# Seven products for three parts of each down projection, with weight sums on GpSimd

## The chip, the cores and the metric

The kernel runs on one core of a Trainium2 chip. The metric is the device time of one execution in microseconds. A core has a matrix engine (TensorE, PE in the profile; PEld is its weight load), a vector engine (VectorE, DVE), a scalar engine (ScalarE, ACT), GpSimd (POOL) and SyncE (SP), which here only issues DMAs. Each works through its own queue in order; semaphores order them among each other. PE reads operands from the on-chip memory SBUF and accumulates into PSUM banks of 512 fp32 columns.

## What is computed

One decoder layer on x of 512 tokens by 1024 channels, in fp32: a SwiGLU feed-forward (FFN 1), a mixer (three groups of dilated attention heads beside a gated linear recurrence), and a second FFN 2, each between two RMS norms. The change concerns the FFNs alone:

```python
def swiglu(x, w_gate, w_up, w_down):
    return (jax.nn.silu(x @ w_gate) * (x @ w_up)) @ w_down

f = swiglu(rms_norm(h, ffn1_norm_pre[l]), ffn1_w_gate[l], ffn1_w_up[l], ffn1_w_down[l])
h = h + 0.5 * rms_norm(f, ffn1_norm_post[l])
```

The hidden width D_FF is 2816, 22 blocks of 128. The down projection multiplies a 512 x 2816 activation by a 2816 x 1024 weight.

## The kernel before

Every fp32 operand is split into a high part in the format fp32r (ACT copies it) and a low part, the difference (DVE subtracts): `split`, lines 268 to 270. A product is three matmuls, high by high, high by low and low by high; `mm3` and `tokens` write these out.

Weights come from HBM in one stream of 1 MB tiles `raw` (two buffers, `raw_of`, loads issued on SP at L215), in an order that `stream_plan` fixes from the same events that drive the loops. Split weights lie in `w8` buffers (four of 1024 columns, high and low), smaller ones in `w4`.

Each FFN goes through 22 blocks f of the hidden width. For the first ones (five in FFN 1, three in FFN 2) gate and up are ordinary products on 512 columns (L282 to L284). For the others gate and up are computed together by `seven` (lines 583 to 622): the product of 2 x 2 blocks with seven block products instead of eight (Winograd's form of Strassen's scheme). Its inputs are sums of activation quarters, formed once per FFN, and sums of weight quarters, formed for each f by `w_forms` (lines 564 to 581): four DVE adds of 512 columns (L570, L571, L572, L575), then three splits of 1024 and one of 512. Its seven products are 84 matmuls on 256 columns (L594 to L596). The products p1, p6 and p7 go on adding in one PSUM bank; in between ACT copies that bank out (L601), and DVE makes the four results of such copies and other products (L606). `prod` then applies SiLU and the product and splits the result u into the activation tiles `act`.

The down projection is cut along the hidden width in five parts, `FF_PARTS` (four of 4 blocks, one of 6). `down(a, half)` multiplies part a for 512 of the 1024 output columns: for each of four token blocks 12 matmuls on 512 columns (L388 to L390, `tokens`), with the activations as stationary and the weights as moving operand. Its weights are split into the buffers `wd` (two). The result is copied (part 0, L662, ACT) or added (L664, DVE) into the SBUF accumulator `facc`. The halves of a part are spread over the gate/up products of the next part. The last part ends the FFN in `last_product`, with squares, norm and residual.

The order on each engine is set by a planner: it goes through the program with a cost for each instruction, and of the instructions that are ready on an engine by these costs it puts the one with the best priority next. Priority is the place in the program; `high_priority(offset)` moves a block ahead by so many places, here 100 for weights (`AHEAD`) and 200 for evacuations (`EVAC`). On the chip an engine follows that fixed order, and an instruction that isn't ready holds up what is behind it. Tiles of one tag share its buffers, and a new tile waits until the users of an old one are done.

The order of events in an FFN (`ffn_order`, lines 49 to 66) lists `std`, `prep` (the weight forms of one f, one product ahead), `prod` (with the halves of the part before) and `down`.

Of the kernel before, what the change touches and what calls it, by code (L numbers as in the profile page):

```python
# [10 lines left out]
F32 = mybir.dt.float32  # L11
F32R = mybir.dt.float32r
# [4 lines left out]
P = 128  # L17
# [3 lines left out]
NF = 22  # L21
FF_PARTS = ((0, 4), (4, 8), (8, 12), (12, 16), (16, 22))
NSTD = {1: 5, 2: 3}
NG = 3
NH = 4
EPS = 1e-6
# [22 lines left out]
def ffn_order(n):  # L49

    order = [("std", f) for f in range(NSTD[n])]
    early = NSTD[n] >= FF_PARTS[0][1]
    order.append(("prep", NSTD[n]))
    if early:
        order.append(("down", 0, 0))
    for a, (f0, f1) in enumerate(FF_PARTS):
        fs = range(max(f0, NSTD[n]), f1)
        halves = () if a == 0 else (1,) if a == 1 and early else (0, 1)  # L60
        for i, f in enumerate(fs):
            if f + 1 < NF:
                order.append(("prep", f + 1))
            c, k = len(fs), len(halves)
            order.append(("prod", f, a - 1, halves[i * k // c:(i + 1) * k // c]))
    return order


# [5 lines left out]
def stream_plan():  # L74

    plan = []

    def down(n, a, half):
        for kk in range(part_blocks(a)):
            plan.append((("down", n, a, half, kk), 1024))  # L80

    def ffn(n):
        for ev in ffn_order(n):
            if ev[0] == "std":
                plan.append((("gate", n, ev[1]), 1024))
                plan.append((("up", n, ev[1]), 1024))
            elif ev[0] == "prep":
                plan.append((("gu", n, ev[1]), 2048))
            elif ev[0] == "down":
                down(n, *ev[1:])  # L90
            else:
                for half in ev[3]:
                    down(n, ev[2], half)
# [36 lines left out]
    ffn(2)  # L130
    return plan

# [24 lines left out]
def hybrid_layer(ctx: ExitStack, tc: tile.TileContext, xT: bass.AP, xN: bass.AP, wst: bass.AP,  # L157
                 first: bass.AP, rows: bass.AP, consts: bass.AP, bias: bass.AP, out: bass.AP):
    nc = tc.nc
    DVE, ACT, PE = nc.vector, nc.scalar, nc.tensor  # L160
# [234 lines left out]

    def gains(pool, *ids):

        t = pool.tile([P, 2, D], F32, name="gains", tag="wd", bufs=2)
# [162 lines left out]

    spool = [None]

    def w_forms(key):

        with tc.high_priority(offset=AHEAD):
            raw = raw_of(key)
            u0, u1, g0, g1 = (raw[:, i * 512:(i + 1) * 512] for i in range(4))
            s12 = spool[0].tile([P, 2, 512], F32, name="s12", tag="s", bufs=2)
            DVE.tensor_add(s12[:, 1, :], u0, u1)  # L570
            DVE.tensor_add(s12[:, 0, :], s12[:, 1, :], g0)  # L571
            DVE.tensor_add(u0, u0, g0)  # L572
# [50 lines left out]

    def ffn(n, x, r, forms_x, apool, pss):
        t, steps = forms_x
        acts = {}

        def act_at(f):

            if f // 4 not in acts:  # L630
                at = apool.tile([P, 8, T], F32R, name="act", tag="act", bufs=3)
                acts[f // 4] = Act([at[:, j, :] for j in range(4)], [at[:, 4 + j, :] for j in range(4)])
            return acts[f // 4].hi[f % 4], acts[f // 4].lo[f % 4]

        def part(a):
            f0, f1 = FF_PARTS[a]
            his, los = zip(*(act_at(f) for f in range(f0, f1)))
            return Act(his, los)

        def std_out(psg, psu, f):  # L640

            g, u = tmp("g"), tmp("u")
            if r is None:
                ACT.activation(g, psg, AF.Silu)
                DVE.tensor_mul(u, psu, g)
            else:
                DVE.tensor_mul(g, psg, r)
                ACT.activation(g, g, AF.Silu)
                DVE.tensor_mul(u, psu, r)
                DVE.tensor_mul(u, u, g)  # L650
            split(*act_at(f), u)

        def wd():
            return apool.tile([P, 2, 1024], F32R, name="wd", tag="wd", bufs=2)

        def down(a, half):
            ws = [fetch(("down", n, a, half, kk), wd, AHEAD) for kk in range(part_blocks(a))]
            for b in range(4):
                ps, y = acc_ps(), fb(b, FHALVES[half])
                tokens(ps, ws, part(a), b)  # L660
# [2 lines left out]
                else:  # L663
                    DVE.tensor_add(y, ps, y)  # L664

        def prod(f, w, a, hs_):
            g, u = tmp("g"), tmp("u")
            seven(t, w, aux_ps()[:, :HB], [g[:, h] for h in HALVES], [u[:, h] for h in HALVES])
            for half in hs_:
                down(a, half)  # L670
            ACT.activation(g, g, AF.Silu)
            DVE.scalar_tensor_tensor(u, g, -1.0, u, op0=ALU.mult, op1=ALU.mult)
            split(*act_at(f), u)

        keys = [(w, n, i) for i in range(NSTD[n]) for w in ("gate", "up")]
        forms = {}
        for ev in ffn_order(n):
# [6 lines left out]
                if j < len(steps):  # L684
                    steps[j]()
            elif ev[0] == "prep":
                forms[ev[1]] = w_forms(("gu", n, ev[1]))
            elif ev[0] == "down":
                down(ev[1], ev[2])
            else:  # L690
                prod(ev[1], forms.pop(ev[1]), ev[2], ev[3])
        a = len(FF_PARTS) - 1
        return lambda half, kk: ("down", n, a, half, kk), part_blocks(a), part(a)


    def act_two(pool):

        ts = [pool.tile([P, 8, T], F32R, name="act", tag="act", bufs=3) for _ in range(2)]
        return Act([ts[0][:, k, :] for k in range(8)], [ts[1][:, k, :] for k in range(8)])

    def spare(pool):

        def pair():
            t = pool.tile([P, 8, T], F32R, name="act", tag="act", bufs=3)
            return [t[:, 4 * i:4 * i + 4, :].rearrange("p (s k) t -> p s (k t)", s=2) for i in range(2)]

        def one():
            return tx_slot(pool).rearrange("p s k t -> p s (k t)")

        both = []  # L710

        def of_pair():
            if not both:
                both.extend(pair())
            return both.pop(0)

        return [of_pair, of_pair, one, w8]

    ff1 = ExitStack()
    ap1 = ff1.enter_context(tc.tile_pool(name="act1", bufs=1))  # L720
    new_h()
    u1 = act_two(ap1)
    acc = npool.tile([P, T], F32, name="acc", tag="acc", bufs=1)
    warm(eps)

# [31 lines left out]
        if b >= 2:  # L757
            bd1.turn(b - 2)

    last_product(*end1, True, grow1, spare(ap1), block1)  # L760
    ff1.close()


# [226 lines left out]
    with ExitStack() as mx:  # L990
# [144 lines left out]
        for c in range(KC):  # L1135
# [5 lines left out]


    ap2 = ctx.enter_context(tc.tile_pool(name="act2", bufs=1))
    u_t = [ap2.tile([P, 8, T], F32R, name="act", tag="act", bufs=3) for _ in range(2)]
    his, los = ([t[:, 0:4, :], t[:, 4:8, :]] for t in u_t)
# [4 lines left out]
    slots = spare(ap2)  # L1150
# [3 lines left out]
    pss = gemm_first(keys[:NFIRST], u2, [spare(ap2)[2]],  # L1154
                     {3: [lambda: bd2.turn(2)], 4: [lambda: bd2.turn(3)]})
    end2 = ffn(2, u2, None, forms_of(u2, his, los, ap2, True), ap2, pss)
    new_h()
# [57 lines left out]
def _block(key, a):  # L1215
# [3 lines left out]
    if kind in ("down", "out"):  # L1219
        if kind == "out":  # L1220
            w, r0, half = a["w_out"], key[2] * 2 * P, key[1]
        else:
            w, r0, half = a[f"ffn{key[1]}_w_down"], (FF_PARTS[key[2]][0] + key[4] * 2) * P, key[3]
        return w[r0:r0 + 2 * P, half * T:(half + 1) * T].reshape(2, P, T).transpose(1, 0, 2)
    if kind == "gu":
        u, g = (_cols(a[f"ffn{key[1]}_w_{k}"], key[2] * P) for k in ("up", "gate"))
        return np.concatenate([u, g], axis=1)
# [54 lines left out]
```

## Time and profile before

| | |
|---|---|
| median of 3 runs (lowest, highest) | 1245.29 us (1245.27, 1245.92) |
| the profiled execution | 1245.37 us, of which the span is 1243.6 us |
| granted PE clock | 0.998 |
| window 57 to 320 us, the products of FFN 1 | 263.00 us: PE busy 263.00, DVE 200.85, ACT 128.42, POOL 2.91 |
| window 905 to 1218 us, those of FFN 2 | 313.00 us: PE busy 313.00, DVE 233.73, ACT 153.47, POOL 3.43 |

The span runs from the first to the last instruction; the little beside it is start and end. Busy times of an engine in a window are the time in which at least one of its instructions runs. Consecutive matmuls and consecutive DVE instructions overlap by their ends, so what a further one costs is the distance from start to start, not its duration. In the timeline a row is: start, duration, engine, line, operation, output<-inputs by tile names, shapes, count, and in brackets idle time before it with what ended it. In the groups a row ends with busy time, mean duration in ns, and idle time before with the releasers. `w`, `wd`, `raw`, `s` are weight tiles (split, split for down, loaded, sums), `acc` and `aux` are PSUM banks.

### The profile page before, as it was taken

The page shows a single profiled execution, that of the slowest core. Times are in us where ns is not written, and L with a number is a line of the kernel's source. Part 1 is how long each engine was busy: PE and PEld are TensorE (multiplying, and loading weights), DVE is VectorE, ACT ScalarE, POOL GpSimd, SP SyncE. Part 2 cuts the span into 40 slices and gives each one's busy share as a digit, 9 for nine tenths or more (in the row PEclk, how much of TensorE's full clock was granted, in tenths as well). Part 3 has the DMA queues.
Part 4 walks back from the last instruction along what each step waited for, and adds up shares of the span by engine and source line. Part 5 has one row for each costly group of instructions (what it writes and reads, how often), then busy time and mean ns, then how long its engine had stood idle before and what let it go on. Part 6 is the DMA issues. An engine that isn't in the chain of part 4 may idle for free.

```text
span 1243.6 us, 19076 instructions
## 1 busy us (share of the span) xinstructions
PE 1232.1 (99%) x7748; PEld 1117.6 (90%) x7748; DVE 930.4 (75%) x1473; ACT 664.3 (53%) x1100; POOL 26.2 (2%) x51
## 2 busy tenths in 40 slices
PE   9999999999999999999999999999999999999997
PEld 8899999999878899999988887888899999999986
DVE  7996777796576588888575898864798667777755
ACT  7555444455355365666544788734565544445432
POOL 0000000000002000000000000000100000000000
PEclk9999999999999999999999999999999999999999
DMA  6222222235424223222243222224443222222241
GB/s 242 102 79 103 101 102 102 101 126 184 167 90 144 85 95 103 77 89 91 100 172 102 70 99 102 102 102 169 142 130 136 103 103 102 103 103 73 103 182 67
DMA packets 27383, 141.37 MB, mean 114 GB/s; under 512 B 2976, under 2 KB 6176, under 8 KB 13216
## 3 DMA queue, kind: packets, MB, share of 16 engines
q1 hardware_dynamic: 20016, 122.86, 27.9%
q0 software_dynamic: 7280, 17.30, 4.1%
q8 instruction: 60, 0.98, 0.3%
q14 instruction: 27, 0.22, 0.1%
HBM read 129.67 MB, written 6.29 MB: 109 GB/s over the span
## 4 chain that ended last, share of the span: by engine, by line
PE 89%; DVE 6%; ACT 4%; issue 1%; DVEq 0%; ACTq 0%
PE acc L594 11%; PE acc L595 11%; PE acc L596 11%; PE acc L388 7%; PE acc L389 7%; PE acc L390 7%; PE acc L282 6%; PE acc L283 6%; PE acc L284 6%; PE aux L595 3%; PE aux L594 3%; PE aux L596 3%; PE acc L793 1%; PE acc L795 1%; PE acc L794 1%
## 5 line engine op out<-in xcount | busy, mean ns | idle before, releaser
L270 DVE TENSOR_TENSOR w<-raw,w 128x1024 fp32r<-128x1024 f32 (+1 forms) x241 | 257.9, 1074 | 97.2 <-ACT w L269 64.7
L269 ACT ACTIVATE w<-raw 128x1024 fp32r<-128x1024 f32 (+1 forms) x241 | 225.2, 938 | 181.3 <-DVE raw L575 61.0
L594 PE MATMUL acc<-big,w 128*128 128x256 f32 x896 | 255.4, 285 | 0.0
L595 PE MATMUL acc<-big,w 128*128 128x256 f32 x896 | 254.4, 284 | 0.0
L596 PE MATMUL acc<-big,w 128*128 128x256 f32 x896 | 254.1, 284 | 0.0
L594 PEld LDWEIGHTS acc<-big,w 128*128 128x128 f32 x896 | 171.6, 192 | 1.0
L595 PEld LDWEIGHTS acc<-big,w 128*128 128x128 f32 x896 | 171.7, 192 | 0.6
L596 PEld LDWEIGHTS acc<-big,w 128*128 128x128 f32 x896 | 171.7, 192 | 0.0
L601 ACT ACTIVATE c<-acc 128x256 f32<-128x256 f32 x172 | 65.2, 379 | 81.4 <-PE acc L596 78.1
L389 PE MATMUL acc<-wd,act 128*128 128x512 f32 x256 | 99.8, 390 | 0.0
L388 PE MATMUL acc<-wd,act 128*128 128x512 f32 x256 | 99.6, 390 | 0.0
L390 PE MATMUL acc<-wd,act 128*128 128x512 f32 x256 | 99.4, 389 | 0.0
L594 PE MATMUL aux<-big,w 128*128 128x256 f32 x288 | 81.5, 283 | 0.0
L595 PE MATMUL aux<-big,w 128*128 128x256 f32 x288 | 81.5, 283 | 0.0
L596 PE MATMUL aux<-big,w 128*128 128x256 f32 x288 | 81.4, 283 | 0.0
L594 PE MATMUL acc<-tx,w 128*128 128x256 f32 x272 | 77.2, 284 | 0.0
L596 PE MATMUL acc<-tx,w 128*128 128x256 f32 x272 | 77.0, 283 | 0.0
L595 PE MATMUL acc<-tx,w 128*128 128x256 f32 x272 | 77.0, 283 | 0.0
L282 PE MATMUL acc<-big,w 128*128 128x512 f32 x192 | 74.7, 389 | 0.0
L283 PE MATMUL acc<-big,w 128*128 128x512 f32 x192 | 74.7, 389 | 0.0
L284 PE MATMUL acc<-big,w 128*128 128x512 f32 x192 | 74.7, 389 | 0.0
L270 DVE TENSOR_TENSOR w<-s,w 128x1024 fp32r<-128x1024 f32 x52 | 63.7, 1224 | 10.2 <-ACT w L269 10.1
(316 smaller groups left out, 2753.0 us busy)
## 6 DMA issues: line engine op xcount, KB each, us to landing
raw<-in_w SPq DMA_DIRECT2D x110, 1024.0 KB, 4.8
big<-act POOLq DMA_DIRECT2D x6, 512.0 KB, 3.4
gains<-in_rows POOLq DMA_DIRECT2D x5, 512.0 KB, 5.0
h<-in_x SPq DMA_DIRECT2D x8, 256.0 KB, 5.0
h<-in_xn POOLq DMA_DIRECT2D x4, 512.0 KB, 7.6
kept_m<-h POOLq DMA_DIRECT2D x4, 512.0 KB, 2.9
h<-kept_m POOLq DMA_DIRECT2D x4, 512.0 KB, 5.4
kept<-h POOLq DMA_DIRECT2D x4, 512.0 KB, 3.4
```

The costliest lines, as they stand in the source:

```text
L269: ACT.activation(dh, src, AF.Copy)
L270: DVE.tensor_sub(dl, src, dh.bitcast(F32))
L282: PE.matmul(ps, wh, xh, start=first, stop=False)
L283: PE.matmul(ps, wh, xl, start=False, stop=False)
L284: PE.matmul(ps, wl, xh, start=False, stop=last)
L388: PE.matmul(ps, x.hi[k][:, bl], wh, start=k == 0, stop=False)
L389: PE.matmul(ps, x.hi[k][:, bl], wl, start=False, stop=False)
L390: PE.matmul(ps, x.lo[k][:, bl], wh, start=False, stop=k == x.n - 1)
L594: PE.matmul(ps, wh, xh, start=start and k == 0, stop=False, skip_group_check=True)
L595: PE.matmul(ps, wh, xl, start=False, stop=False, skip_group_check=True)
L596: PE.matmul(ps, wl, xh, start=False, stop=k == 3, skip_group_check=True)
L601: ACT.activation(c, ps, AF.Copy)
```

## The change

Parts 1, 2 and 3 of each down product (blocks 4 to 16) are each computed in seven products. A part is taken as 2 x 2 blocks: two token halves of 256 by two halves of its hidden width (256 each) times two by two blocks of weights (256 by 512). `down7` has 7 products of 12 matmuls on 512 columns, in place of 96 such matmuls; the weights move and the activations are stationary, as before.

- Weights of a part come as two 1 MB tiles (`dg`). `d_forms` makes four sums of 1024 columns on GpSimd and seven splits of 1024: four ahead of the gate/up product before, three (`rest`) after the first product of the down7.
- Activation sums are made when the gate/up results come (`into`): for the first two blocks of a part a difference, for the other two three further sums and a split of 1024.
- The bank that p1, p6 and p7 share is added up over the three parts: after each of them its contents are put into SBUF tiles `e` (part 1: ACT copies, later: DVE adds), and four adds of 1024 columns on DVE put them into `facc` at the end of part 3. The other products are added into `facc` directly. That makes 14 evacuations of 512 columns a part, in place of 8.
- The down product of a part now stands in one piece, behind the first gate/up product of the next part (part 0: both halves in a row), and no weight forms of a further gate/up product are made ahead at that place.
- `w_forms` makes its four sums on GpSimd for f from 8 on (`LATE`), on DVE before.
- The activation tiles lie elsewhere: tags `e`, `wd` (one buffer, shared with the gains), `tt` and `xf` (four buffers) in place of `act` and the two `wd` buffers. The ordinary down parts split their weights into `w8`.

```diff
+SEVEN = (1, 2, 3)
+LATE = 8
...
+    ready = False
+    for f in range(NSTD[n], NF):
+        if f - 1 in firsts and f == NSTD[n]:
+            order += down(firsts[f - 1])
+        if not ready:
+            order.append(("prep", f))
+        ready = f + 1 < NF and f not in firsts
+        if ready:
+            order.append(("prep", f + 1))
+        if f in firsts and firsts[f] in SEVEN:
+            order.append(("prepd", firsts[f]))
+        order.append(("prod", f))
+        if f in firsts:
+            order += down(firsts[f])
...
-            DVE.tensor_add(s12[:, 1, :], u0, u1)
-            DVE.tensor_add(s12[:, 0, :], s12[:, 1, :], g0)
-            DVE.tensor_add(u0, u0, g0)
+            add = (POOL if late else DVE).tensor_add
+            add(s12[:, 1, :], u0, u1)
+            add(s12[:, 0, :], s12[:, 1, :], g0)
+            add(u0, u0, g0)
...
-            DVE.tensor_add(g1, s12[:, 0, :], g1)
+            add(g1, s12[:, 0, :], g1)
...
+            if i < 2:
+                put(tt[:, 2:4, :].rearrange("p k t -> p (k t)"))
+                split(x["x0"][:, 0, j, :], x["x0"][:, 1, j, :], tt[:, 2, :])
+                DVE.tensor_sub(tt[:, 0, :], tt[:, 2, :], tt[:, 3, :])
+                return
+            u = tmp("u")
+            put(u)
+            split(x["x1"][:, 0, j, :], x["x1"][:, 1, j, :], u)
+            DVE.scalar_tensor_tensor(tt[:, 1, :], u[:, HB:], -1.0, tt[:, 0, :], op0=ALU.mult, op1=ALU.subtract)
+            DVE.tensor_sub(tt[:, 3, :], u[:, HB:], tt[:, 3, :])
+            DVE.scalar_tensor_tensor(tt[:, 2, :], tt[:, 1, :], -1.0, u[:, :HB], op0=ALU.mult, op1=ALU.subtract)
+            x["t", j] = f32r_big().rearrange("p s t -> p (s t)").rearrange("p (s k t) -> p s k t", s=2, k=4)
+            split(x["t", j][:, 0], x["t", j][:, 1], tt)
...
+            with tc.high_priority(offset=AHEAD):
+                (u0, g0), (u1, g1) = ([r_[:, :1024], r_[:, 1024:]]
+                                      for r_ in (raw_of(("dg", n, a, 0)), raw_of(("dg", n, a, 1))))
+                sd, rd = half_sum(), half_sum()
+                POOL.tensor_add(sd, u0, u1)
+                POOL.tensor_add(rd, sd, g0)
+                form("p1", g0)
+                form("p2", g1)
+                form("p6", rd)
+                form("p5", sd)
+
+            def rest():
+                with tc.high_priority(offset=AHEAD):
+                    POOL.tensor_add(u0, u0, g0)
+                    form("p7", u0)
+                    form("p4", u1)
+                    POOL.tensor_add(g1, rd, g1)
+                    form("p3", g1)
...
+        def product(p, to, start, put):
+                for i in range(2):
+                    if start:
+                        to[i] = aux_ps() if to is z else acc_ps()
+                    il = slice(i * P, (i + 1) * P)
+                    for j in range(2):
+                        xh, xl = (v[:, il] for v in xs(p, j))
+                        wh, wl = (w[p][:, q, j * T:(j + 1) * T] for q in range(2))
+                        PE.matmul(to[i], xh, wh, start=start and j == 0, stop=False, skip_group_check=True)
+                        PE.matmul(to[i], xh, wl, start=False, stop=False, skip_group_check=True)
+                        PE.matmul(to[i], xl, wh, start=False, stop=j == 1, skip_group_check=True)
+                    with tc.high_priority(offset=EVAC):
+                        put(i, to[i])
...
+            product("p1", b, True, keep(0))
+            rest()
+            product("p2", y, True, out_of(0, 0, ALU.add))
+            product("p6", b, False, keep(1))
+            product("p5", z, True, out_of(2, 1, ALU.subtract))
+            product("p7", b, False, keep(2))
+            product("p4", y, True, out_of(0, 1, ALU.subtract))
+            product("p3", z, False, out_of(2, 0, ALU.add))
+            if a == SEVEN[-1]:
+                for o, half, q, op in ((0, 0, 0, ALU.add), (2, 0, 1, ALU.add), (0, 1, 2, ALU.subtract),
+                                       (2, 1, 2, ALU.subtract)):
+                    dst = facc[:, 2 * o + half:2 * o + half + 3:2, :]
+                    DVE.tensor_tensor(dst, dst, e[:, q], op=op)
```

More of the change, by code (lines that the diff above doesn't have):

```diff
@@ L53, in ffn_order, with down @@
     order = [("std", f) for f in range(NSTD[n])]
[L54 to L65, printed above, removed]
+    firsts = {f0: a - 1 for a, (f0, _) in enumerate(FF_PARTS) if a}
+    def down(a):
+        return [("down7", a)] if a in SEVEN else [("down", a, 0), ("down", a, 1)]
+    ready = False
[12 more added lines that the diff above has]
+            order += down(firsts[f])
     return order
@@ L90, in ffn @@
                 down(n, *ev[1:])
[L91 to L93 removed]
+            elif ev[0] == "prepd":
+                for i in range(2):
+                    plan.append((("dg", n, ev[1], i), 2048))
         for half in range(2):
@@ L159, in hybrid_layer @@
     nc = tc.nc
-    DVE, ACT, PE = nc.vector, nc.scalar, nc.tensor
+    DVE, ACT, PE, POOL = nc.vector, nc.scalar, nc.tensor, nc.gpsimd
     cpool = ctx.enter_context(tc.tile_pool(name="cpool", bufs=1))
@@ L625, in ffn, with f32r_big, part_of @@
         t, steps = forms_x
-        acts = {}
-        def act_at(f):
[L630 to L633, printed above, removed]
+        acts, sevens = {}, {}
+        def f32r_big():
+            return apool.tile([P, 4, T], F32R, name="xf", tag="xf", bufs=4)
+        def part_of(f):
+            return next(a for a, (f0, f1) in enumerate(FF_PARTS) if f < f1)
@@ L640, in std_out @@
         def std_out(psg, psu, f):
-            g, u = tmp("g"), tmp("u")
+            g = tmp("g")
             if r is None:
                 ACT.activation(g, psg, AF.Silu)
[L645 to L654, printed above, removed]
+                into(f, lambda dst: DVE.tensor_mul(dst, psu, g))
+                return
@@ L656, in down @@
+            u = tmp("u0")
+            DVE.tensor_mul(g, psg, r)
+            ACT.activation(g, g, AF.Silu)
+            DVE.tensor_mul(u, psu, r)
+            into(f, lambda dst: DVE.tensor_mul(dst, u, g))
         def down(a, half):
-            ws = [fetch(("down", n, a, half, kk), wd, AHEAD) for kk in range(part_blocks(a))]
+            ws = [fetch(("down", n, a, half, kk)) for kk in range(part_blocks(a))]
             for b in range(4):
@@ L664, in down, with prod @@
                     DVE.tensor_add(y, ps, y)
-        def prod(f, w, a, hs_):
+        def prod(f, w):
             g, u = tmp("g"), tmp("u")
             seven(t, w, aux_ps()[:, :HB], [g[:, h] for h in HALVES], [u[:, h] for h in HALVES])
-            for half in hs_:
-                down(a, half)
             ACT.activation(g, g, AF.Silu)
-            DVE.scalar_tensor_tensor(u, g, -1.0, u, op0=ALU.mult, op1=ALU.mult)
-            split(*act_at(f), u)
+            into(f, lambda dst: DVE.scalar_tensor_tensor(dst, g, -1.0, u, op0=ALU.mult, op1=ALU.mult))
@@ new lines, in d_forms, with half_sum, form @@
+        def d_forms(a):
+            def half_sum():
+                return apool.tile([P, 1024], F32, name="sd", tag="s", bufs=2)
+            w = {}
+            def form(name, src):
+                w[name] = w8()
+                split(w[name][:, 0, :], w[name][:, 1, :], src)
+            with tc.high_priority(offset=AHEAD):
[15 more added lines that the diff above has]
+                    form("p3", g1)
+            return w, rest
@@ new lines, in down7, with xs, keep, put @@
+        def down7(a, w, rest):
+            x = sevens.pop(a)
+            if "e" not in sevens:
+                sevens["e"] = apool.tile([P, 3, 2, T], F32, name="esum", tag="e", bufs=1)
+            e, new = sevens["e"], a == SEVEN[0]
+            b, y, z = {}, {}, {}
+            def xs(p, j):
+                if p in ("p1", "p2", "p3"):
+                    v = x["x0"] if p == "p1" else x["x1"]
+                    o = HB if p == "p3" else 0
+                    return v[:, 0, j, o:o + HB], v[:, 1, j, o:o + HB]
+                k = {"p5": 0, "p6": 1, "p4": 2, "p7": 3}[p]
+                return x["t", j][:, 0, k, :], x["t", j][:, 1, k, :]
+            def product(p, to, start, put):
+                for i in range(2):
+                    if start:
[9 more added lines that the diff above has]
+                        put(i, to[i])
+            def keep(q):
+                def put(i, ps):
+                    if new:
+                        ACT.activation(e[:, q, i, :], ps, AF.Copy)
+                    else:
+                        DVE.tensor_add(e[:, q, i, :], ps, e[:, q, i, :])
+                return put
+            def out_of(o, half, op):
+                def put(i, ps):
+                    dst = fb(i + o, FHALVES[half])
+                    if a:
+                        DVE.tensor_tensor(dst, dst, ps, op=op)
+                    else:
+                        ACT.activation(dst, ps, AF.Copy, scale=1.0 if op == ALU.add else -1.0)
+                return put
+            product("p1", b, True, keep(0))
[11 more added lines that the diff above has]
+                    DVE.tensor_tensor(dst, dst, e[:, q], op=op)
@@ L696, in act_two, with of @@
     def act_two(pool):
-        ts = [pool.tile([P, 8, T], F32R, name="act", tag="act", bufs=3) for _ in range(2)]
-        return Act([ts[0][:, k, :] for k in range(8)], [ts[1][:, k, :] for k in range(8)])
+        ts = [pool.tile([P, 4, T], F32R, name="xf", tag="xf", bufs=4) for _ in range(4)]
+        return ts[:2], ts[2:]
     def spare(pool):
[L703 to L717, printed above, removed]
+        def of(t):
+            return t[:, 0:4, :].rearrange("p (s k) t -> p s (k t)", s=2)
+        return {"e": lambda: of(pool.tile([P, 6, T], F32R, name="act", tag="e", bufs=1)),
+                "tt": lambda: of(pool.tile([P, 4, T], F32R, name="act", tag="tt", bufs=1)),
+                "xf": lambda: of(pool.tile([P, 4, T], F32R, name="xf", tag="xf", bufs=4)),
+                "tx": lambda: tx_slot(pool).rearrange("p s k t -> p s (k t)")}
     ff1 = ExitStack()
@@ L1143, in hybrid_layer @@
     ap2 = ctx.enter_context(tc.tile_pool(name="act2", bufs=1))
-    u_t = [ap2.tile([P, 8, T], F32R, name="act", tag="act", bufs=3) for _ in range(2)]
-    his, los = ([t[:, 0:4, :], t[:, 4:8, :]] for t in u_t)
+    his, los = act_two(ap2)
     u2 = act_of(his, los)
```

58 lines of the change are left out of this document (48 added, 10 removed).

## The prediction

> **What bounds the kernel now.** I read the page's busy times and slices first, then the chain that ended last and the waits of PE, and then the stage that the change touches.
>
> ```profile
> span 1243.6 us, 19076 instructions
> PE 1232.1 (99%) x7748; PEld 1117.6 (90%) x7748; DVE 930.4 (75%) x1473; ACT 664.3 (53%) x1100; POOL 26.2 (2%) x51
> PE 89%; DVE 6%; ACT 4%; issue 1%; DVEq 0%; ACTq 0%
> ...
> PE aux L728 <- DVE eps L201: 1.1, 1, 1.1
> PE aux L282 <- ACT rec L269: 0.9, 1, 0.9
> PE aux L283 <- DVE rec L270: 0.5, 1, 0.5
> PE aux L448 <- DVE u L440: 0.4, 2, 0.3
> ```
>
> PE is busy for 99% of the span, the chain is 89% PE, and these four rows are all of PE's waits: 2.9 us, none in an FFN loop. A matmul taken out of those loops is time taken out, as long as the weight forms and evacuations still come in time. What decides is therefore how near DVE is to PE there. Four gate/up products and two halves of a down product make one period; here it is (first row), with two of its products and one half (the other rows).
>
> ```profile
> core 0: us, PE busy (x) PEld busy (x) DVE busy (x) ACT busy (x) POOL busy (x), PEclk, DMA share, GB/s
> 144.43:206.69 62.26, 62.26 (x434) 58.42 (x433) 46.91 (x69) 28.44 (x44) 0.00 (x0) 1.00 0.29 102
> ...
> 154.50:164.60 10.10, 10.10 (x86) 10.07 (x85) 9.62 (x13) 6.64 (x11) 0.00 (x0) 1.00 0.36 116
> 164.60:175.56 10.96, 10.96 (x51) 9.07 (x50) 9.30 (x15) 2.97 (x4) 0.00 (x0) 1.00 0.42 172
> ```
>
> The clock is 1.00. PE never stops; DVE has 46.91 of 62.26 us, and GpSimd does nothing.
>
> **The gain on PE.** Before, a part of the down product has 2 halves x 4 blocks x 4 k x 3 = 96 matmuls on 512 columns; with seven products it has 7 x 2 blocks x 2 k x 3 = 84, of the same form (weights moving, activations as 128x128 stationary operand). Busy means overlap, so I take start to start:
>
> ```profile
> 200.57 0.39 PE L388 MATMUL acc<-wd,act 128*128 128x512 f32 x1
> ...
> 203.97 0.39 PE L388 MATMUL acc<-wd,act 128*128 128x512 f32 x1
> ...
> 207.04 0.28 PE L594 MATMUL acc<-big,w 128*128 128x256 f32 x1
> ...
> 208.24 0.28 PE L595 MATMUL acc<-big,w 128*128 128x256 f32 x1
> ```
>
> The first two lie 15 matmuls apart: 3.40 / 15 = 0.2267 us. The last two lie 10 apart: 0.12 us, so a gate/up product (84 of them) takes 10.1 us. Twelve matmuls less in 3 parts of 2 FFNs: 72 x 0.2267 = **16.3 us**. A period goes to 62.26 - 2.72 = 59.5 us; a down7 within it takes 84 x 0.2267 = 19.0 us.
>
> **DVE.** Steps, again start to start:
>
> ```profile
> 163.56 0.42 DVE L606 TENSOR_TENSOR u<-c 128x256 f32<-128x256 f32 x1
> 163.90 0.42 DVE L606 TENSOR_TENSOR u<-acc,c 128x256 f32<-128x256 f32 x1
> ...
> 168.58 0.68 DVE L664 TENSOR_TENSOR facc<-acc,facc 128x512 f32<-128x512 f32 x1
> 169.19 0.68 DVE L571 TENSOR_TENSOR s<-s,raw 128x512 f32<-128x512 f32 x1
> 169.78 0.68 DVE L572 TENSOR_TENSOR raw<-raw 128x512 f32<-128x512 f32 x1
> 170.38 1.22 DVE L270 TENSOR_TENSOR w<-raw,w 128x1024 fp32r<-128x1024 f32 x1
> 171.52 0.69 DVE L664 TENSOR_TENSOR facc<-acc,facc 128x512 f32<-128x512 f32 x1
> ```
>
> So 256 columns cost 0.34, 512 cost 0.60 and 1024 cost 1.14, whether an operand is in PSUM (acc) or not. A gate/up product now has 4 sums (2.40), low parts of 3 x 1024 and 1 x 512 (4.02), 4 evacuations of 256 (1.36), the SwiGLU product (0.60) and the activation's low part (0.60): 8.98. Without the sums it is 6.58. In the seven-product parts the last 0.60 becomes 0.68 for the first two f (low part and difference, 256 each) and 2.76 for the other two (0.60 + 3 x 0.34 + 1.14): 6.66 and 8.74. A down7 has 7 low parts of 1024 (7.98) and 14 evacuations of 512 (8.40), against 4 and 8 before. In a period of parts 2 and 3 DVE thus has 2 x 6.66 + 2 x 8.74 + 16.4 = **47.2 us**, and had DVE kept the sums (16 x 0.60 + 4 x 1.14 = 14.2) it would have 61.4, over PE's 59.5. Of the 47.2, 12.5 read PSUM (14 x 0.60, and 3 x 0.34 per product); the other 34.7 take both operands from SBUF.
>
> **GpSimd.** From f = 8 on it gets four 512 sums a product, and four 1024 sums a down7: 24 sums' worth of 512 a period. No row shows GpSimd computing on a tile. Its own rows, and the slowest row of that shape on any engine:
>
> ```profile
> L815 POOL DMA_DIRECT2D vals<-vals x16 | 7.9, 501 | 6.7 <-PE aux L448 3.9 <-ACT vals L803 2.7
> L1272 POOL MEMSET const-float32-0.0<- 128x1 f32 x1 | 0.1, 100 | 0.2 <-issue 0.2
> L570 DVE TENSOR_TENSOR s<-raw 128x512 f32<-128x512 f32 x52 | 35.6, 685 | 0.4 <-DMA raw<-in_w 0.4
> L1118 DVE TENSOR_TENSOR_SCAN th<-gt 128x512 f32<-128x512 f32 x8 | 9.7, 1218 | 0.0
> POOL h L748 <- PE acc L596: 300.7, 1, 300.7
> ```
>
> A sum costs GpSimd between 0.60 (as on DVE) and 1.22 (the scan row). I take 1.22: that GpSimd is DVE's equal would be an assumption in the change's favour. That is 24 x 1.22 = 29.3 us a period, half of GpSimd's time, so its own queue holds; the sums must stand ahead of the load of h (last row), at whose head POOL waits 300.7 us today, and they are ready earlier than it is. By the Trainium skill, GPSIMD Engine Reference, section Performance versus the Vector engine, an add of 2048 fp32 columns takes 4497 ns there; a quarter, 1.12 us, is an estimate from that page, and the forecast below would be 1247 with it. No run here shows it yet.
>
> What counts is what these 29.3 us do to DVE. Ends: nothing (DVE 47.2, PE leads; less than nothing is excluded, since PE already sets the time) and one after the other (47.2 + 29.3 = 76.5, 17.0 over PE). PE leads by 12.3, so the sums stay hidden only while less than 42% of them stand in DVE's way. I take the instructions that fetch both operands from the memory GpSimd works in as those that can't run beside a sum: 34.7 of 59.5 us, 58%, hence 17.0 us, DVE at 64.2, **4.7 us over PE a period**. This is a judgement between the ends, and it carries the forecast. The Trainium skill, SBUF — State Buffer, section SBUF: two separate sides, says that a VectorE instruction with two SBUF inputs and a GpSimd instruction share one port pair as an exclusive lock for a whole instruction. It speaks against this change and for the one-at-a-time reading; no trace here shows it.
>
> Four such periods (parts 2 and 3, two FFNs): 18.8 us. In part 1's periods DVE still does the sums of f = 6 and 7 (4.8), ACT takes 6 of the 14 evacuations, and GpSimd has 16 sums' worth (19.5): 30.8 + 4.8 + 12.8 + 0.58 x 19.5 = 59.7, 0.2 over, 0.4 for both. Part 4's five products: 5 x 6.58 + 0.58 x 19.5 = 44.2 against 50.4 on PE: hidden. The chain sums kept over the parts end in 4 adds of 1024 per FFN, 4.6 us on DVE just after a period where DVE is last; part 4's 6.2 us of room hides some; ends 0 and 9.2 for both FFNs, I take the middle, 4.6.
>
> **The rest of the change.** These come at nothing, each with its cover:
>
> ```profile
> L269 ACT ACTIVATE wd<-raw 128x1024 fp32r<-128x1024 f32 x4 | 4.2, 1047 | 0.0
> raw<-in_w SPq DMA_DIRECT2D x110, 1024.0 KB, 4.8
> SPq L215 <- DVE w L270: 403.0, 45, 18.7
> ```
>
> ACT gets three more weight halves and about two more 1024 of activations: 28.44 + 5 x 1.05 = 33.7 of 59.5 us. SP's loads are as many and as large; but a down7 holds both raw tiles at once, so the next load leaves only when the p7 form is split. That form needs the buffer of p1, free 12 x 0.2267 = 2.7 us into the down7, and 1.05 + 1.14 = 2.2 us for its two halves; load 4.8, three sums 3.7, split 2.2: the next product's forms stand at 15.6 of 19.0 us. The room is 3.4 us, more for the forms it uses later; without it PE waits at the head of the next product, and behind a late form wait ACT's later splits and evacuations. PSUM: a chain's bank is added to again two products after its evacuation was due (5.4 - 1.4 = 4 us, against 0.60). x0 of the next part waits for p1 of the down7, the first product: 1.4 to 2.7 us of ACT and DVE, both with other work queued at higher priority. The tiles in new homes (act3 beside the gains, e, tt, xf) are used when their former users are done.
>
> **Sum**, against the profiled execution's 1245.37 (span 1243.6; the median of the runs shown is 1245.29): 1245.4 - 16.3 + 18.8 + 0.4 + 4.6 = **1252.9, say 1253 us**.
>
> **Rivals.** *A, the sums are hidden.* GpSimd's sums don't slow DVE; DVE stays at 47.2 of 59.5 and PE never waits: 1245.4 - 16.3 = 1229. For it: ACT and DVE split tiles side by side today at steady durations, and PE's waits are nil with DVE at 9.62 of 10.10 us in a product. Against it: the margin is gone at 42% of interference. It holds 1228 to 1233 (products 6 and 7, where DVE has 2.40 + 8.74 = 11.1 against 10.1, may cost 2 us per FFN). It is the case on the other side. *C, only the handover fails.* DVE keeps up, but the 3.4 us of room before the next product is used up, about 2 us at each of six down7: 1229 + 12 = 1241, range 1234 to 1247. It decides from sums that come more than 3.4 us late. *D, fully one after the other*: 17.0 x 4 + 9.2 = 77 more than A, 1306; for it only that sums and low parts meet in every product, against it that 12.5 us of DVE's work read PSUM and that DVE waits for ACT at times anyway.
>
> **How the numbers follow.** B, the forecast, has 0.54: its own range is 1240 (a sum at 1.08 us, the kept sums' adds hidden: 25.9 x 0.58 + 47.2 - 59.5 = 2.7 a period) to 1280 (interference at 79%, DVE's whole share of the period: 10.9 a period, and 9.2). A 0.25, C 0.13, D 0.08. What a measurement can tell from no change is 0.2%, 2.5 us. Faster than 1242.8: A's 0.25, 0.10 of C, 0.02 of B: 0.37. Within: 0.03 of C and 0.06 of B: 0.09. Slower: 0.46 of B and D's 0.08: 0.54. For 8 in 10 the range must take in A below and most of B above: 1228 to 1275; outside remain D, B's tail (0.07) and a little below A.
>
> **What would show it.** Right: in periods of parts 2 and 3 the window is some 64 us long, PE waits for the weight forms' low parts (L270), mean durations of two-operand DVE rows rise where POOL is busy while those reading PSUM stay, and GpSimd's 512 sums show about 1.2 us. Wrong: periods of 59.5 us with DVE near 47 us and no PE wait (A); PE waits only at the first product after a down7 (C). It fails if GpSimd's sum is much dearer or cheaper than 1.22, or if DVE is slowed by less than 42% of it.

## The result, and the profile after

The changed kernel takes 1317.03 us (median of 4 runs, 1315.88 to 1318.42) against 1245.28: ratio 1.0576, 95% interval 1.0558 to 1.0594. The forecast was 1253 with a range to 1275: the direction is right, the size is not.

The page of the changed kernel, in the same lines as before:

```profile
span 1313.7 us, 19235 instructions
PE 1243.8 (95%) x7676; PEld 1123.6 (86%) x7676; DVE 1042.2 (79%) x1471; ACT 695.5 (53%) x1142; POOL 275.8 (21%) x187
PE 62%; DVE 20%; ACT 7%; issue 5%; DMA 3%; POOL 2%; DVEq 0%; ACTq 0%; POOLq 0%
```

The 72 matmuls are gone (7748 to 7676), yet PE is busy 11.7 us longer and idle 58 us longer (1313.7 - 1243.8 = 69.9 us, against 11.5). Its waits, by who was waited for (total us, times, longest):

```profile
PE acc L605 <- ACT c L612: 26.7, 21, 3.0
PE aux L605 <- ACT c L612: 26.3, 6, 4.4
PE acc L398 <- ACT xf L279: 5.5, 2, 2.9
```

L605 is the first of the three matmul lines in `seven`, L612 the copy out of PSUM that frees the bank for it, L398 a matmul of the last down product. None of these waits was there before. The windows of the periods of parts 2 and 3 in FFN 1, and most of part 4's five products (columns as in the prediction's table):

```profile
151.11:222.22 71.11, 63.35 (x421) 58.88 (x420) 62.70 (x71) 32.82 (x50) 36.35 (x22) 0.95 0.25 89
222.22:293.30 71.08, 64.28 (x422) 60.03 (x421) 66.33 (x72) 33.10 (x50) 38.13 (x21) 0.93 0.26 90
293.30:345.00 51.70, 45.86 (x362) 44.84 (x361) 44.65 (x46) 26.13 (x43) 26.32 (x18) 0.97 0.29 102
```

A period takes 71.1 us where I had 64.2, and neither PE (63.35) nor DVE (62.70) fills it. The granted clock is 0.93 to 0.97 in these windows, where it was 1.00. The groups show who was slowed (mean ns is the number after the busy time):

```profile
L581 POOL TENSOR_TENSOR s<-raw 128x512 f32<-128x512 f32 x28 | 42.9, 1530 | 115.8 <-DMA raw<-in_w 101.5 <-DVE g L617 14.3
L583 POOL TENSOR_TENSOR raw<-raw 128x512 f32<-128x512 f32 x28 | 53.6, 1913 | 0.0
L744 POOL TENSOR_TENSOR sd<-raw 128x1024 f32<-128x1024 f32 x6 | 14.7, 2453 | 63.9 <-DVE u L727 42.4 <-DMA raw<-in_w 21.5
L617 DVE TENSOR_TENSOR u<-c 128x256 f32<-128x256 f32 x40 | 23.0, 575 | 5.4 <-ACT c L612 5.4
L694 DVE SCALAR_TENSOR_TENSOR tt<-u,tt 128x256 f32<-128x256 f32 x12 | 15.7, 1308 | 0.2
L280 DVE TENSOR_TENSOR xf<-u,xf 128x512 fp32r<-128x512 f32 x24 | 32.6, 1357 | 0.0
L803 DVE TENSOR_TENSOR facc<-facc,acc 128x512 f32<-128x512 f32 x24 | 15.8, 678 | 2.1 <-PE acc L787 2.1
```

DVE's 256-column instructions with both operands in SBUF go from 420 ns to 575 (u<-c) and stand at 1308 (tt<-u); one of 512 columns takes 1357 in place of some 686. The one that reads PSUM (facc<-facc,acc) takes 678, as ever. One place, the product before a down7, shows how that reaches PE. The timeline, all four engines:

```profile
190.32 2.41 POOL L744 TENSOR_TENSOR sd<-raw 128x1024 f32<-128x1024 f32 x1 [10.66 <-DMA raw<-in_w]
192.81 2.46 POOL L745 TENSOR_TENSOR sd<-sd,raw 128x1024 f32<-128x1024 f32 x1
195.24 2.52 POOL L753 TENSOR_TENSOR raw<-raw 128x1024 f32<-128x1024 f32 x1
...
190.43 2.59 DVE L694 SCALAR_TENSOR_TENSOR tt<-u,tt 128x256 f32<-128x256 f32 x1
192.94 2.62 DVE L695 TENSOR_TENSOR tt<-u,tt 128x256 f32<-128x256 f32 x1
195.49 2.82 DVE L280 TENSOR_TENSOR xf<-u,xf 128x512 fp32r<-128x512 f32 x1
198.23 0.41 DVE L696 SCALAR_TENSOR_TENSOR tt<-tt,u 128x256 f32<-128x256 f32 x1
...
198.68 1.06 ACT L279 ACTIVATE xf<-tt 128x1024 fp32r<-128x1024 f32 x1 [6.62 <-DVE tt L696]
199.64 0.36 ACT L612 ACTIVATE c<-aux 128x256 f32<-128x256 f32 x1
...
195.37 0.28 PE L607 MATMUL acc<-big,w 128*128 128x256 f32 x1
200.06 0.39 PE L605 MATMUL aux<-big,w 128*128 128x256 f32 x1 [4.41 <-ACT c L612]
201.06 0.41 PE L605 MATMUL aux<-big,w 128*128 128x256 f32 x1
201.27 0.41 PE L606 MATMUL aux<-big,w 128*128 128x256 f32 x1
```

Three sums follow each other on GpSimd, and each of three DVE instructions starts with one of them and ends just after it. The fourth then takes its usual 0.41. At the head of its queue ACT waits 6.62 us for DVE's result; behind it is the PSUM copy that PE needs, and PE stops for 4.41 us. After that matmuls on 256 columns start 0.21 us apart in place of 0.12 for a while: the granted clock from 200.7 to 203.9 us is 0.50. Six stops of this kind, 4.3 to 4.4 us each, stand just before the six down7; they are the second of PE's waits above.

In the first product after each down7 PE stops too, six times for 1.6 to 3.0 us (14.8 in all), and there ACT is held by something else. One of them:

```profile
228.32 1.26 POOL L586 TENSOR_TENSOR raw<-s,raw 128x512 f32<-128x512 f32 x1 [1.23 <-DVE w L280]
229.62 0.63 ACT L279 ACTIVATE w<-raw 128x512 fp32r<-128x512 f32 x1 [3.21 <-POOL raw L586]
230.57 0.39 PE L605 MATMUL acc<-big,w 128*128 128x256 f32 x1 [2.44 <-ACT c L612]
```

ACT waits 3.21 us for GpSimd's fourth sum of a product's weights, which itself had to wait for DVE; the PSUM copy is again behind it. So the sums cost in two ways: they hold up DVE's instructions, and they come late for their own reader.

### The profile page after: what moved, and what is told of

It is laid out like the page before. It is cut to its first block, busy times and chain, and to the rows that moved or that the text cites. A ratio compares the mean times of both kernels' runs of the same rounds, so it can differ in the third digit from the quotient of the medians.

```text
span 1313.7 us, 19235 instructions
## 1 busy us (share of the span) xinstructions
PE 1243.8 (95%) x7676; PEld 1123.6 (86%) x7676; DVE 1042.2 (79%) x1471; ACT 695.5 (53%) x1142; POOL 275.8 (21%) x187
## 4 chain that ended last, share of the span: by engine, by line
PE 62%; DVE 20%; ACT 7%; issue 5%; DMA 3%; POOL 2%; DVEq 0%; ACTq 0%; POOLq 0%
DVE w L280 8%; PE acc L605 7%; PE acc L606 7%; PE acc L607 7%; PE acc L292 5%; PE acc L293 5%; PE acc L294 5%; DMA raw<-in_w 3%; PE acc L400 3%; PE acc L398 3%; PE acc L399 3%; DVE xf L280 2%; ACT w L279 2%; POOL raw L586 1%; PE aux L605 1%
## 5 line engine op out<-in xcount | busy, mean ns | idle before, releaser
L280 DVE TENSOR_TENSOR w<-raw,w 128x1024 fp32r<-128x1024 f32 (+1 forms) x279 | 325.7, 1171 | 102.9 <-ACT w L279 90.6
L279 ACT ACTIVATE w<-raw 128x1024 fp32r<-128x1024 f32 (+1 forms) x279 | 264.1, 953 | 208.6 <-PE acc L294 48.2
L605 PE MATMUL acc<-big,w 128*128 128x256 f32 x896 | 258.4, 288 | 17.2 <-ACT c L612 17.2
L606 PE MATMUL acc<-big,w 128*128 128x256 f32 x896 | 257.6, 287 | 0.0
L607 PE MATMUL acc<-big,w 128*128 128x256 f32 x896 | 257.3, 287 | 0.0
L605 PEld LDWEIGHTS acc<-big,w 128*128 128x128 f32 x896 | 175.2, 196 | 19.2 <-ACT c L612 18.8
L606 PEld LDWEIGHTS acc<-big,w 128*128 128x128 f32 x896 | 175.1, 195 | 0.4
L607 PEld LDWEIGHTS acc<-big,w 128*128 128x128 f32 x896 | 175.1, 195 | 0.0
L605 PE MATMUL aux<-big,w 128*128 128x256 f32 x288 | 85.2, 296 | 26.3 <-ACT c L612 26.3
L612 ACT ACTIVATE c<-acc 128x256 f32<-128x256 f32 x172 | 64.6, 376 | 52.9 <-PE acc L607 50.3
L605 PE MATMUL acc<-tx,w 128*128 128x256 f32 x272 | 79.0, 291 | 9.6 <-ACT c L612 9.4
L607 PE MATMUL aux<-big,w 128*128 128x256 f32 x288 | 84.4, 293 | 0.0
L606 PE MATMUL aux<-big,w 128*128 128x256 f32 x288 | 84.4, 293 | 0.0
L605 PEld LDWEIGHTS aux<-big,w 128*128 128x128 f32 x288 | 58.1, 202 | 27.5 <-ACT c L612 27.5
L410 POOL DMA_DIRECT2D gains<-in_rows x5 | 2.8, 560 | 363.1 <-issue 224.2
L280 DVE TENSOR_TENSOR w<-s,w 128x1024 fp32r<-128x1024 f32 x52 | 74.0, 1422 | 5.0 <-ACT w L279 4.9
L279 ACT ACTIVATE w<-s 128x1024 fp32r<-128x1024 f32 x52 | 54.9, 1055 | 24.7 <-POOL s L582 9.9
```

Source lines behind the costliest of these rows:

```text
L279: ACT.activation(dh, src, AF.Copy)
L280: DVE.tensor_sub(dl, src, dh.bitcast(F32))
L605: PE.matmul(ps, wh, xh, start=start and k == 0, stop=False, skip_group_check=True)
L606: PE.matmul(ps, wh, xl, start=False, stop=False, skip_group_check=True)
L607: PE.matmul(ps, wl, xh, start=False, stop=k == 3, skip_group_check=True)
L612: ACT.activation(c, ps, AF.Copy)
```

## The experiments

Theory 1 is that a GpSimd sum and a DVE instruction with two SBUF operands run one at a time, and that this reaches PE by the queues. Theory 2: the seven-product structure itself, its order and its handovers, stops PE. Theory 3: GpSimd's sums are only late for their own readers. In the ratios below the kernel before is 1.

**e1: all sums on DVE.**

```diff
-LATE = 8
+LATE = 99
...
-                POOL.tensor_add(sd, u0, u1)
+                DVE.tensor_add(sd, u0, u1)
```

(and so for the other three sums of `d_forms`)

> All sums of the changed kernel back on DVE (LATE = 99, the four sums of a down7 too), GpSimd computes nothing. Theory 1 (a GpSimd sum and a DVE instruction with two SBUF operands run one at a time; DVE falls behind, then ACT's queue, then PE, and PE's clock drops after each stop): DVE has 61.4 us of work in a period of parts 2 and 3 against 59.5 on PE, so 1229 + 4 x 1.9 + up to 9 for the kept sums: 1237 to 1250 us; DVE rows back to the durations of before (w<-s 1226 ns, u<-c 420 ns), clock 0.998, no PE wait of 4.4 us. Theory 2 (the seven-product structure itself, its order and its handovers, stops PE, whoever makes the sums): still above 1295 us with most of the 58 us of PE idle time. Theory 3 (GpSimd's sums are only late for those that wait for them, DVE is not slowed by them): 1237 to 1250 us, but DVE's durations as in the changed kernel.

Measured: 1258.87 us, 1.0107 (1.0083 to 1.0132). 58 of the 72 us (1317.0 less 1245.3) come back, and DVE's durations with them. It is 9 us above the upper end of theory 1, and the clock of the profiled execution is 0.991, not 0.998: the new order costs something too. v1, below, shows where.

**e2: the gate/up sums on DVE, the down sums on GpSimd** (the first edit of e1 alone), and **e3: the reverse** (the second alone).

> Only the sums of the gate/up weights (f from 8 on) go back to DVE; the four sums of 1024 of each down7 stay on GpSimd. Theory 1: the wait of 4.4 us at the end of the product before a down7 stays (six times, each with some 2 us of lost clock behind it: about 39 us), the rest goes: 1265 to 1285 us. Theory 2: above 1295 us. Theory 3: no DVE row is longer than before.

> Only the four sums of 1024 of each down7 go back to DVE; the gate/up sums from f = 8 on stay on GpSimd. Theory 1: the six waits of 4.4 us go, the 2.5 us waits behind a down7 and the small ones stay: 1317 - 39 = about 1278 us (1265 to 1290). Theory 2: above 1295 us. Together e2 and e3 must each give back part of the 72 us, and the two parts should add up to about what e1 gives back.

Measured: e2 1286.72, 1.0333 (1.0318 to 1.0348); e3 1302.72, 1.0457 (1.044 to 1.0475). They give back 30 and 14 us, together 44.6, not e1's 58. Both lie above theory 1's ranges, e2 by 2 us and e3 by 13, and e3 lies where theory 2 had put it (above 1295). Which DVE rows are slow follows from which sums GpSimd makes: tt<-u stands at 1288 ns in e2 and at 421 in e3, w<-s at 1485 in e3 (1224 before). Theory 3 expected no longer row in e2. PE's longest waits, first e2, then e3:

```profile
PE aux L605 <- ACT c L612: 16.3, 4, 4.3
PE acc L785 <- DVE esum L796: 13.0, 2, 6.7
```

```profile
PE acc L605 <- ACT c L612: 37.7, 25, 4.3
PE aux L605 <- ACT c L612: 7.7, 2, 4.4
```

With the down sums alone on GpSimd, six long stops are there: four just before a down7, and, inside the down7 of part 3, one of 6.3 us in FFN 1 and one of 6.7 us in FFN 2, where PE waits until DVE has added the bank of p1 into `e`. With the gate/up sums alone on GpSimd all six stops before a down7 are gone, as expected. But the six in the first product after a down7 grow from 14.8 us to 23.4, and two of 3.3 and 4.4 us appear in part 4's products (the second row of e3); before each of these eight ACT waits for the late fourth sum.

**e4: GpSimd's sums left out**, and nothing else; **e8: the same, with the last down part in another order.** The second edit, in `last_product` and `tokens`:

```diff
+            held = {}
+            if x.n == 6 and half == 0:
+                for b in range(3):
+                    held[b] = acc_ps()
+                    tokens(held[b], ws, x, b, ks=range(5))
             for b in range(4):
-                ps = acc_ps()
-                tokens(ps, ws, x, b, fills.get((half, b), lambda: None))
+                if b in held:
+                    ps = held[b]
+                    tokens(ps, ws, x, b, ks=(5,))
+                else:
+                    ps = acc_ps()
+                    tokens(ps, ws, x, b, fills.get((half, b), lambda: None))
```

> All sums that GpSimd makes in the changed kernel are left out (the splits read the raw weights in their place, so the outputs are not the reference's); nothing else changes. Theories 1 and 3: PE never stops for weights, DVE has 47.2 us in a period of 59.5: 1229 to 1235 us, clock 0.998, no wait of PE over 1 us in the FFN loops. Theory 2: above 1290 us, with PE waits at the same places.

> e4 (GpSimd's sums left out, so the outputs are not the reference's) with one more edit: in the last down part of each FFN the first three token blocks are multiplied for five of the six hidden blocks first, and for the last one afterwards. If the 3.2 us that PE stops there in e4 come from waiting for the activation of f = 21, twice, with some 2 us of lower clock behind each: 1240.5 - 10 = about 1230 us, which is the 1229 that the matmuls alone give. If the rest of the 11 us lies elsewhere: above 1236 us.

Measured: e4 1240.51, 0.9959 (0.9944 to 0.9974); e8 1231.3, 0.9886 (0.9871 to 0.9901). Theory 2 as the main cause falls. But e4 is above its 1235, and e8 shows by what. The end of FFN 1 in e4 (timeline):

```profile
316.98 1.06 ACT L279 ACTIVATE tx<-raw 128x1024 fp32r<-128x1024 f32 x1 [5.81 <-DMA raw<-in_w]
317.94 0.61 ACT L729 ACTIVATE g<-g 128x512 f32<-128x512 f32 x1
...
320.61 0.80 PE L398 MATMUL acc<-w,xf 128*128 128x512 f32 x1 [3.17 <-ACT xf L279]
```

The SiLU of the last block f = 21 stands in ACT's queue behind a split that waits for its weight tile to land, and the last product runs out of activations after five of six blocks. The kernel before had half a down product between that SiLU and the last product (`halves` of f = 21); the change moved it away. With other matmuls put there (in program order 15 on each of three token blocks, 10 us at the 0.2267 us of the prediction, in place of one block's 15) e8 comes to some 2 us above the 1229 of the matmuls alone. PE's row in e8: fewer busy us than in the changed kernel by 29.0, with the same matmuls.

```profile
PE 1214.8 (99%) x7676; PEld 1102.9 (90%) x7676; DVE 935.9 (76%) x1471; ACT 702.8 (57%) x1142; POOL 26.1 (2%) x51
```

**e5: the kernel before, with GpSimd additions that nobody waits for; e6 with memsets, e7 with copies in their place.** Behind the split of b in `w_forms`:

```diff
+            if key[0] == "gu" and key[2] >= 8:
+                for _ in range(4):
+                    nc.gpsimd.tensor_add(s12[:, 0, :], s12[:, 0, :], s12[:, 1, :])
```

(e6: `memset(s12, 0.0)`; e7: `tensor_copy(s12[:, 0, :], s12[:, 1, :])`)

> The kernel before, with four GpSimd additions of 512 columns added to every gate/up product from f = 8 on (112 in all, as many as the changed kernel has there). They work on the sums tile after its last use, and no result needs them. Theory 1 (port held for a whole instruction): DVE rows with two SBUF operands get longer (w<-s from 1226, u<-c from 420 ns), those that read PSUM (facc<-acc 687 ns) do not; a period has 45.3 us of DVE and 20 us of GpSimd against 62.3 of PE, so some PE waits: 1247 to 1275 us. Theory 3 (lateness only): nothing waits for them, so 1245 us and DVE's durations as before.

> As e5, but the four GpSimd instructions a product are memsets of the tile (1024 columns each): GpSimd writes SBUF and reads nothing. If it is the reading that gets in DVE's way: 1245 us and DVE's durations as before. If any GpSimd instruction does: as e5, in proportion to GpSimd's busy time.

> As e5, but each of the four GpSimd instructions a product is a copy of 512 columns: one operand read from SBUF, one written. If reading SBUF at all holds the port for the whole instruction: DVE's two-operand rows get longer as in e5, by GpSimd's shorter time: between 1246 and 1270 us. If only instructions with two operands do: 1245 us and DVE's durations as before.

Measured: e5 1280.82, 1.0284 (1.0266 to 1.0301); e6 1245.86, 1.0004 (0.9994 to 1.0013); e7 1247.73, 1.0018 (1.0009 to 1.0027). e5 is 6 us above my range, e7 at the lower end of its own. The groups, first of e5, then e6, then e7:

```profile
L579 POOL TENSOR_TENSOR s<-s 128x512 f32<-128x512 f32 x112 | 197.6, 1765 | 413.7 <-DVE w L270 407.1
L609 DVE TENSOR_TENSOR u<-c 128x256 f32<-128x256 f32 x40 | 47.4, 1184 | 4.3 <-ACT c L604 4.3
L667 DVE TENSOR_TENSOR facc<-acc,facc 128x512 f32<-128x512 f32 x48 | 32.8, 686 | 4.0 <-PE acc L390 4.0
```

```profile
L579 POOL MEMSET s<- 128x1024 f32 x112 | 107.0, 955 | 466.5 <-DVE w L270 461.6
L609 DVE TENSOR_TENSOR u<-c 128x256 f32<-128x256 f32 x40 | 16.8, 420 | 4.3 <-ACT c L604 4.3
```

```profile
L579 POOL COPY s<-s 128x512 f32<-128x512 f32 x112 | 122.3, 1092 | 454.0 <-DVE w L270 448.8
L609 DVE TENSOR_TENSOR u<-c 128x256 f32<-128x256 f32 x40 | 28.2, 706 | 4.3 <-ACT c L604 4.3
```

No result depends on these additions, no wait of DVE or ACT on GpSimd is in e5's trace, and the kernel before becomes 36 us slower: theory 3 falls as the whole account. What it names is in the changed kernel all the same, in the stops after each down7. DVE's u<-c goes to 1184 ns beside additions, to 706 beside copies, and stays at 420 beside memsets, which only write; facc<-acc, with an operand in PSUM, stays at 686 beside additions. The rows w<-s that I had expected to grow stay at 1224 ns, because the additions start only behind them. So GpSimd's reading is what blocks, and of these DVE rows only those with two SBUF operands are blocked. That is the first half of theory 1, and the rule of the Trainium skill, SBUF — State Buffer, section SBUF: two separate sides, which I cited with no trace for it: these runs agree with it, in both its limits. In size the copies fall short of it: 122 us of them make DVE 23 us busier, 198 us of additions 81, so part of a copy seems to run beside DVE; why, no run shows.

**v1: e1 with e8's order; v2, v3 and v5: v1 with fewer parts** (`SEVEN = (1, 2)`, `(2, 3)` and `(1,)`).

> e1 (all sums on DVE) with the same edit of the last down part: 1258.9 - 10 = about 1249 us. What remains over 1229 is DVE's 61.4 us in periods of 59.5, and lost clock. Below 1245 only if the two effects share waits.

> v1 with only parts 1 and 2 in seven products (part 3 ordinary, both halves in one piece). Matmuls: 48 fewer than before, 1245.3 - 10.9 = 1234. If what keeps v1 at 1247 is DVE at 61.4 us in a period of 59.5, then one overfull period a FFN is left, with an ordinary one of 47 us in 62 behind it: 3 to 6 us of waits, 1237 to 1241 us, faster than before by some 0.4%. If the seven-product order costs a wait at every part: 1245 or more.

> v1 with only parts 2 and 3 in seven products (part 1 ordinary). Again 1234 for the matmuls alone. The wait of 1 to 2 us at products 6 and 7 goes with part 1's extra forms; the two overfull periods stay, back to back: 1238 to 1245 us, no better than v2 by DVE's load.

> v1 with part 1 alone in seven products. Matmuls: 24 fewer than before, 1245.3 - 5.4 = 1239.9. Its period has 30.8 + 9.6 + 12.8 + 4.6 = 57.8 us of DVE (six of the evacuations are ACT's) against 59.5 on PE, so by DVE's load only the wait of some 1.4 us at products 6 and 7 is left, once a FFN, and the chain sums' adds: 1241 to 1244 us, the first of these versions below the kernel before. If the down parts in one piece cost by themselves (their order, not DVE's load): 1245 or more.

Measured: v1 1247.08, 1.0015 (1.0006 to 1.0025); v2 1244.58, 0.9999 (0.999 to 1.0008); v3 1248.98, 1.0027 (1.0015 to 1.0038); v5 1242.71, 0.9979 (0.9969 to 0.9989). v1 is near the 1249 I had said, and e8's order gives 11.8 us back: what e1 lay above theory 1 was the end of the FFNs. v2 and v3 miss their ranges by 4 us: of the 10.9 us of matmuls saved v2 keeps less than one, and v3 loses more than all of them, to waits of 1 to 1.8 us and to a clock of 0.995 (v3). Only with part 1 alone, where DVE needs 57.8 of 59.5 us by the sum in the expectation, is the kernel faster than before, by 0.2%. That fits DVE's load as the limit, but no run separates the load from the order. v5's page:

```profile
PE 1226.2 (99%) x7724; PEld 1112.3 (90%) x7724; DVE 963.6 (78%) x1515; ACT 681.6 (55%) x1122; POOL 26.2 (2%) x51
```

## Why the prediction failed, step by step

The runs divide the result: 1245.3 - 16.3 (matmuls, as predicted) + 2.2 (e8 over the 1229.1 that this leaves) + 9.2 (e4 less e8, the end of the FFNs) + 76.5 (changed kernel less e4, the sums on GpSimd) = 1316.9. The last three are differences between runs, so the sum closes by construction. I had 23.8 us for the last term and nothing for the one before.

- **The gain on PE, 16.3 us**: right; e8 has 14.0 of it.
- **GpSimd's price, 1.22 us**: right to 7%. The shortest sums take 1.26 to 1.30 us, those of 1024 columns 2.4 to 2.5. The means of 1.53 to 1.91 are longer: sums wait for DVE too (one at 224.82 us takes 2.28 us, beside a DVE low part from 224.22 to 225.94). The estimate of 1.12 us from the Trainium skill, GPSIMD Engine Reference, section Performance versus the Vector engine, is further off.
- **58% of it in DVE's way**: right as a total. DVE is busy 1042.2 us against 936.4 with the same DVE instructions and no sums (e4): 105.8 us longer. The prediction's own numbers give 0.58 x (4 x 29.3 + 4 x 19.5) = 113. That is partly luck: GpSimd is busy 249.7 us with the sums, not 195.2, and DVE is held for 42% of that.
- **"PE leads by 12.3, so the sums stay hidden only while less than 42% of them stand in DVE's way"**: this step failed. I took the room of a whole period off the blocked time. The room lies elsewhere in the period: sums come three in a row as soon as a weight tile lands, three DVE instructions lose 2.2 us each, and ACT's queue passes that on to a PSUM copy for which PE has less than 3 us (the 24 matmuls of p7 and p4, 0.12 us each). PE then waits for that copy (L612), not, as I had said, for a low part of the weight forms. In place of 23.8 us the sums cost 76.5, which also holds the stops behind late sums and the lost clock. It shows best where I found next to no deficit: part 1's period took 68.2 us (first gate/up matmul at 82.87, next period at 151.11) where I had 59.7, and part 4's five products 59.1 (293.19 to 352.25) where I had 50.4.
- **The clock** was missing as a term. Span and mean granted clock of the changed kernel, then of e8:

```profile
core 0: 1313.7 us, clock 0.979
```

```profile
core 0: 1228.4 us, clock 0.998
```

PE is busy 29.0 us longer than in e8 for the same matmuls. The clock lacks 0.021 of 1313.7 us, 28 us, in the changed kernel and 0.002 of 1228.4 us, 2.5 us, in e8. So about 30% of the 85 us of span between the two kernels is lost in the slow stretches behind PE's stops.
- **"The rest of the change … at nothing"**: wrong at one place. I listed the handover behind each down7, and not the one at the end of an FFN, where the cover was removed: 9.2 us.
- **DVE with all sums, 61.4 us in a period of 59.5**: I named it as the reason for GpSimd and gave it no price. e1 shows that it is the better choice by 58 us.
- **The rivals**: A holds without the sums (e8), so its condition, not its price, fell. C's stops are there, six in the first product after a down7 and from sums that come late, as its condition says; at 14.8 us they come near the 12 it priced, but they are not the only ones. D, 1306, is the nearest number, for another reason: the periods stayed at 71.1 us, below its 76.5, and the rest came from parts 1 and 4, the clock and the FFN ends. Its chance of 0.08 was too small, and the range should not have ended below it.

What stays open: how the 76.5 us divide between DVE instructions held up and sums that come late, since no run of the changed kernel has one without the other. And why e2 and e3 together give back 13.5 us less than e1: by PE's waits it lies in the stops that grow when one kind of sum is gone, but why they grow is not shown.

## What to carry to other kernels

Before moving a sum from VectorE to GpSimd, count which VectorE instructions take both operands from SBUF: here each could wait for nearly a whole GpSimd addition, and then the price is the delay of one instruction in a chain, not a share of a stage. Room on average hides little if the delays come in a row and an in-order queue with PSUM copies stands behind them. When a change moves work, ask at both ends of the loop what that work was covering; here it was the last SiLU before the last product.

## What the runs showed of the hardware

- GpSimd's memsets cost DVE nothing (112 of 955 ns), its copies little (DVE 23 us busier for 122 us of copies), its two-operand additions much (81 us for 198 us). That copies block less than in proportion to their time was not expected.
- In the FFNs of the changed kernel 12 of the 13 stops of PE of 2.4 us or more were followed by 2.5 to 5.3 us of matmuls at about half pace (256 columns 0.21 us apart in place of 0.12), beginning 0.4 to 1.4 us after the restart; one of 2.90 us at 359.20 us was not. In v3 stops of 1.66 and 1.76 us were followed by such a stretch too; stops of up to 1.94 us in e1, v1 and v5 were not.
